# A hybrid decoder layer on one core: page rows of 512 in two rings, keys and C rows loaded a step ahead, the last tile by halves

## The chip, the cores and the metric

The kernel runs on one core of one Trainium2 chip. Its time is the device time of an execution in microseconds (us). A core has a matrix engine (TensorE, PE in the profile, with its weight loads as PEld), VectorE (DVE), ScalarE (ACT), GpSimd (POOL) and SyncE (SP), which here only issues transfers between the chip's memory and the core's buffer.

## The reference

One layer of a hybrid decoder: a diagonal state space branch (S5) and a gated DeltaNet branch run side by side on the same normalised input, are merged by gates, and a SwiGLU block follows. Everything is float32. 2048 prompt positions with 16 meta tokens ahead, and 8 running sequences of 4 tokens; the width is 1024, the inner width of the SwiGLU 2816.

```python
def layer(x, h_re, h_im, s_gdn, conv_buf, splits, lp):
    hn = rms_norm(x, lp['norm_mix_pre'])
    proj = hn @ lp['w_in']
    ...
    y_s5, h_re_n, h_im_n = s5_mix(u, h_re, h_im, ...)
    gs = jax.nn.gelu(y_s5)
    br_a = (gs @ lp['w_s5_glu_a']) * jax.nn.sigmoid(gs @ lp['w_s5_glu_b'])
    qkv_c, conv_new = short_conv(qkv, conv_buf, lp['gdn_conv_w'])
    ...
    o_seg, S = gdn_segment(q, k, v, g, beta, S)          # in chunks of 64
    o = rms_norm(o, lp['gdn_norm']) * jax.nn.silu(zf)
    br_b = o.reshape(b, l, GDN_VW).astype(x.dtype) @ lp['w_gdn_out']
    mix = (jax.nn.sigmoid(ga) * br_a + jax.nn.sigmoid(gb) * br_b) @ lp['w_out']
    x = x + rms_norm(mix, lp['norm_mix_post'])
    f = rms_norm(x, lp['norm_ffn_pre'])
    f = (jax.nn.silu(f @ lp['w_ffn_gate']) * (f @ lp['w_ffn_up'])) @ lp['w_ffn_down']
    x = x + rms_norm(f, lp['norm_ffn_post'])
    return x, h_re_n, h_im_n, S, conv_new
```

## The kernel before

The prompt is cut into four blocks of 512 columns; block 0 has 48 more (16 meta tokens and 32 sample tokens). Each float32 operand of the large products is split into a high and a low part, and a product is made of three: high by high, high by low, low by high (`mm3`, L157 to L161; in the profile three lines in turn, all of one shape). Weight units of 1024 columns come by `wload` (L131): SP loads `wr`, ACT writes the high part, POOL and DVE write half of the low part each into `wu`, a unit of a ring (`Ring`, L56) over the free places of several pools.

**Five stages** follow each other on PE.

- *Projections*, 0 to 1281 us. `p1` goes through groups of output tiles (u, qkv, gate) and, for each, over two blocks. A block's normalised features stand as "pages" (`pages`, L1247), sixteen tiles of two rows by 560 columns, the pool `pg`: four for the high parts `pgh` and four for the low ones `pgl`, for two blocks at a time. They are made by `p1_features` and `to_features` (L243): transposes on PE into `pst`, high part by ACT, low part by DVE. Beside the products, four queues of generators are advanced by `tick` (L1779) at given rates: features of later blocks, `gdn_alpha` (keys and decay: `kTa`, `E`, the products `psk`, and `Z`, stored to `m_d`), the tables of S5 (`s5_setup`, whose loop over two halves loads rows of C as `ctl`, L1021, and transposes them, L1044), and the chunks of the delta rule (`gdn_chunk` with `px`, `X`, and `o_out` with `pT`, L732). One core's engines work through their own lists in order, which the build fixes: what stands behind a waiting instruction on an engine's list waits too, SP's list of transfers included. All plain loads and stores named here are on SP's list.
- *Merge*, 1281 to 1595 us: products of the S5 outputs and of the DeltaNet outputs with three weights (`psga`, `psgb`, `psgo`). Their inputs are pages again (`p2_prep`, L1251).
- *Way out*, 1595 to 1796 us (`psr`, L1377 to L1380): the merged features are the stationary operand, weights are streamed.
- *Gate and up*, 1796 to 2696 us (`psf`), 348 or 344 columns a product, with sums and differences of operands in big buffers on one side of the core's memory (`gr`, `xp`, `fr`, `ae`, `am0`, `am1`). Results are stored to `h_d`.
- *Down*, 2700 to 3215 us (`down`, `down_tiles` L1630): two halves of the rows, four groups of the inner width. `hr` loads a piece of `h_d`, ACT and DVE split it to `hh` and `hl` (stationary), the streamed operand is the weight unit, and sums collect in `facc`. Twelve weight units lie in `wp3`, in the place of gate and up's buffers, from address 122848 per partition on. After the last group of a row tile its squares are summed (ACT), `rsqrt` (L102 to L109) takes twelve small DVE instructions, one DVE instruction scales the tile, and POOL adds it to `y_prompt` in the chip's memory by an accumulating transfer (L1669).

Of the kernel before, what the change touches and what calls it, by code (L numbers as in the profile page):

```python
# [24 lines left out]
H = 4  # L25
# [17 lines left out]
GW = 348  # L43
PAIRS = ((0, 348), (696, 348), (1392, 344))
# [7 lines left out]
def ap_of(t, off, dims):  # L52
    return bass.AP(tensor=t.tensor, offset=t.offset + off, ap=[list(d) for d in dims])
# [19 lines left out]
class Trunk:  # L73
# [169 lines left out]
    def to_features(self, ys, gain, hi, lo):  # L243
# [4 lines left out]
        for k0 in range(0, 8, 2):  # L248
            ps = self.pt.tile([P, 2, 256], F32, tag="pt", name="pst")
# [323 lines left out]
    def gdn_alpha(self, b):  # L573
# [7 lines left out]
        zs = []  # L581
        for i, (ci, nt, c0) in enumerate(ch):
            kT = self.gd.tile([P, H, P], F32, tag="al", bufs=3, name="kTa")[:, :, :nt]
            nc.sync.dma_start(kT, ap_of(self.qkv_d, 512 * QW + c0, [[QW, P], [P * QW, H], [1, nt]]))
            e = self.decay_load(ci, nt, self.gd.tile([P, H, P], F32, tag="al", bufs=3, name="E"))
# [9 lines left out]
            z = self.gd.tile([P, H, P], F32, tag="al", bufs=3, name="Z")[:nt, :, :nt]  # L595
# [115 lines left out]
    def o_out(self, o, qn, lo, hi, col):  # L711
# [16 lines left out]
        yield  # L728
        pT = self.gp.tile([P, H, P], F32, tag="gp", name="pT")
# [7 lines left out]
    def gdn_chunk(self, ci, c0):  # L737
# [9 lines left out]
        for a in (0, 64):  # L747
            for h in range(H):
                mm(px[a:a + 32, h, 0:32], M[a + 32:a + 64, h, a:a + 32], V[a + 32:a + 64, h])
            v.tensor_copy(X[a:a + 32], px[a:a + 32, :, 0:32])  # L750
# [130 lines left out]
    def s5_setup(self):  # L881
# [118 lines left out]
        nc.sync.dma_start(ld[:16], ap_of(io["s5_D"], 0, [[1, 16], [16, G]]))  # L1000

# [6 lines left out]
        for hf in range(2):  # L1008
# [8 lines left out]
            cts = []  # L1017
            for nm in ("s5_C_re", "s5_C_im"):
                ct = self.c2("ctl")[:, :256].rearrange("p (q k e) -> p q k e", q=2, k=2)
                for k in range(2):  # L1020
                    nc.sync.dma_start(ct[:, :, k], ap_of(io[nm], h0 * 16 * 64, [[64, P], [P * 64, 2], [1, 64]]))  # L1021
                cts.append(ct)
# [25 lines left out]
            for g0 in range(h0, h0 + 16, 4):  # L1048
# [24 lines left out]
                outer(V2, (CR, CI), (R2, R1), "n", 1, 9)  # L1073
                nc.sync.dma_start(self.wv_d[gs, :, 3].rearrange("g p (t c) -> p g t c", c=16), V2)
# [171 lines left out]
    def pages(self, n):  # L1246
        new = lambda nm: [self.pg.tile([P, 2, PW], F32R, tag="pg", name=nm) for _ in range(n)]  # L1247
        return new("pgh"), new("pgl")

    def p2_prep(self, b):  # L1250
# [4 lines left out]
        oh, ol = self.pages(2)  # L1255
# [8 lines left out]
        sh, sl = self.pages(2)  # L1264
# [365 lines left out]
    def down_tiles(self, grp, k0, n, wd, gi, last):  # L1630
        nc, v = self.nc, self.nc.vector
        c0 = grp[0][2]
# [11 lines left out]
        for a, r, c in grp:  # L1644
            both = wide and gi < last
            rr = 2 * r if both else r
            cl = slice(c - c0, c - c0 + rr)
            for half in range(2):
# [7 lines left out]
                if gi == 0:  # L1656
                    nc.scalar.activation(a[:rr, cs], ps, AF.Copy)
                else:
                    v.tensor_add(a[:rr, cs], a[:rr, cs], ps)
            if wide and gi == last - 1:  # L1660
                t = self.lw.tile([SMP, D], F32, tag="lw", name="lows")
                nc.sync.dma_start(t, a[r:2 * r])
                nc.gpsimd.tensor_add(a[:r], a[:r], t)
            if gi == last:
# [4 lines left out]
                nc.gpsimd.dma_start(dst, a[:r], accum_op=OP.add)  # L1669

# [14 lines left out]
    def run(self):  # L1685
# [16 lines left out]
        with ExitStack() as lo:  # L1702
            self.wr = self.pool("wr", 2, lo)
            self.wp.add(self.pool("wp", 3, lo), 3)
            with ExitStack() as pmx, ExitStack() as pgx:
                self.pg = self.pool("pg", 16, pgx, side="right")
# [44 lines left out]
        with ExitStack() as ph:  # L1751
# [9 lines left out]
            self.wp.add(self.pool("wp3", 12, ph, side="right", **kw), 12)  # L1761
# [73 lines left out]
    def p1_features(self, b):  # L1835

        hi, lo = self.pages(4)
        for grp in self.pairs(self.load_tokens(b, True)):
            self.normed(grp, [t for t, _, _ in grp])
            yield  # L1840
            yield from self.to_features(grp, self.g_mix, hi, lo)
        self.xs[b] = hi, lo
# [130 lines left out]
```

## Time and profile before

| what | us |
|---|---|
| median of three runs | 3237.43 (3235.34 to 3238.28) |
| the profiled execution's own time | 3230.07 |
| its span, first to last instruction | 3228.3 |
| PE busy in the span | 3095.1 |
| PE busy in projections, merge, way out, gate and up, down | 1193.95, 302.24, 198.29, 885.52, 515.14 |
| the stages' lengths | 1281, 314, 201, 900, 519, and an end of 13.3 |
| granted clock of PE, mean over the span | 0.978 |

Times below are us from the start of the span of that one execution. A group row reads: line, engine, operation, output and inputs by the program's names, shapes, number of instructions; after the bar the busy time, the mean length in ns, and the idle time just before them with what ended it. A wait row reads: engine and tile with its line, the engine and instruction that ended the wait, total us, times, longest. A window row reads: stretch, its length, busy time of PE, PEld, DVE, ACT, POOL with instructions in brackets, PE's granted clock (1.00 is full), the share of the time that the transfer engines were busy, GB/s. A row of the timeline or of the chain starts with its start and length in us. "SPq" is the issuing of SP's transfers.

### The profile page before, as it was taken

How to read it: one execution, taken by the hardware profiler on the slowest of the kernel's cores; microseconds unless marked ns; L12 is line 12 of the kernel's file. 1: busy time of each engine (PE TensorE's matmuls, PEld its weight loads, DVE VectorE, ACT ScalarE, POOL GpSimd, SP SyncE). 2: the span in 40 equal slices, each digit the busy share in tenths (PEclk: the TensorE clock that was granted, in tenths of full speed). 3: DMA queues.
4: the chain of work that ended last, by engine and by line, in shares of the span. 5: the costliest groups of instructions: out<-in, count | busy, mean ns of one | idle time of the engine just before them, and what ended most of it. 6: DMA issues, size and time to landing. Idle time of an engine off the chain costs nothing.

```text
span 3228.3 us, 47504 instructions
## 1 busy us (share of the span) xinstructions
PE 3095.1 (96%) x17461; PEld 2719.5 (84%) x17461; DVE 2047.1 (63%) x4674; ACT 1127.2 (35%) x1952; POOL 892.9 (28%) x907
## 2 busy tenths in 40 slices
PE   7998989999999999899999899999999999999998
PEld 6887887877777887888788799999999998887776
DVE  6888864557798645644456777777777773245235
ACT  4642222433333224311244444444444444223211
POOL 1133431113332211300211444434434444121110
PEclk9999998999999999999999999999999999999999
DMA  4335556445556645544555533343323335235214
GB/s 120 122 98 164 137 157 179 116 111 141 158 172 180 169 120 149 173 132 134 162 175 190 171 105 105 105 123 106 105 88 105 105 105 174 83 107 133 88 57 70
DMA packets 460552, 419.29 MB, mean 130 GB/s; under 512 B 112330, under 2 KB 384906, under 8 KB 460320
## 3 DMA queue, kind: packets, MB, share of 16 engines
q1 hardware_dynamic: 450048, 382.18, 40.6%
q0 software_dynamic: 10272, 34.09, 3.8%
q8 instruction: 137, 2.24, 0.3%
q14 instruction: 95, 0.78, 0.1%
HBM read 288.27 MB, written 127.65 MB: 129 GB/s over the span
## 4 chain that ended last, share of the span: by engine, by line
PE 67%; DVE 15%; issue 10%; DMA 5%; ACT 2%; POOL 1%; SPq 0%; POOLq 0%; DVEq 0%; ACTq 0%
PE psf L161 9%; PE psf L159 9%; PE psf L160 9%; PE psr L1652 3%; PE psr L1653 3%; PE psr L1655 2%; PE psg L159 2%; PE psg L161 2%; PE psg L160 2%; DVE cy L391 2%; PE psr L1377 2%; PE psr L1378 2%; PE psr L1380 1%; PE psq L159 1%; PE psq L161 1%
## 5 line engine op out<-in xcount | busy, mean ns | idle before, releaser
L159 PE MATMUL psf<-xh,ah 128*128 128x348 f32 (+1 forms) x1848 | 595.0, 322 | 6.2 <-ACT sn L1546 4.5
L160 PE MATMUL psf<-xl,ah 128*128 128x348 f32 (+1 forms) x1848 | 593.8, 321 | 0.0
L161 PE MATMUL psf<-xh,al 128*128 128x348 f32 (+1 forms) x1848 | 593.5, 321 | 0.0
L146 POOL TENSOR_TENSOR wu<-wr,wu 128x512 fp32r<-128x512 f32 x136 | 218.1, 1606 | 690.0 <-ACT wu L144 664.1
L159 PEld LDWEIGHTS psf<-xh,ah 128*128 128x128 f32 x1848 | 348.3, 188 | 8.0 <-ACT sn L1546 5.4
L161 PEld LDWEIGHTS psf<-xh,al 128*128 128x128 f32 x1848 | 348.4, 189 | 0.2 <-DVE al L1486 0.2
L160 PEld LDWEIGHTS psf<-xl,ah 128*128 128x128 f32 x1848 | 348.4, 189 | 0.0
L159 PE MATMUL psg<-pgh,wu 128*128 128x512 f32 (+2 forms) x800 | 301.2, 377 | 1.2 <-ACT gt L1223 1.2
L1652 PE MATMUL psr<-wu,hh 128*128 128x512 f32 (+2 forms) x748 | 295.9, 396 | 3.9 <-ACT hh L1638 3.9
L1653 PE MATMUL psr<-wu,hh 128*128 128x512 f32 (+2 forms) x748 | 295.8, 395 | 0.0
L161 PE MATMUL psg<-pgh,wu 128*128 128x512 f32 (+2 forms) x800 | 290.3, 363 | 4.0 <-DVE wu L147 4.0
L160 PE MATMUL psg<-pgl,wu 128*128 128x512 f32 (+2 forms) x800 | 289.2, 362 | 0.0
L1655 PE MATMUL psr<-wu,hl 128*128 128x512 f32 x704 | 277.3, 395 | 0.0
L147 DVE TENSOR_TENSOR wu<-wr,wu 128x512 fp32r<-128x512 f32 x136 | 121.0, 891 | 130.7 <-ACT wu L144 127.8
L144 ACT ACTIVATE wu<-wr 128x1024 fp32r<-128x1024 f32 x136 | 142.6, 1054 | 133.8 <-DMA wr<-w_ffn_down 48.8
L159 PE MATMUL psq<-pgh,wu 128*128 128x512 f32 (+2 forms) x480 | 183.1, 381 | 4.6 <-ACT gt L1223 4.0
L161 PEld LDWEIGHTS psg<-pgh,wu 128*128 128x128 f32 x800 | 156.0, 195 | 28.7 <-DVE wu L147 4.2
L159 PEld LDWEIGHTS psg<-pgh,wu 128*128 128x128 f32 x800 | 155.8, 195 | 26.6 <-issue 6.1
L160 PE MATMUL psq<-pgl,wu 128*128 128x512 f32 (+2 forms) x480 | 174.4, 363 | 0.0
L161 PE MATMUL psq<-pgh,wu 128*128 128x512 f32 (+2 forms) x480 | 173.7, 362 | 0.0
L1652 PEld LDWEIGHTS psr<-wu,hh 128*128 128x128 f32 (+2 forms) x748 | 138.8, 186 | 39.8 <-ACT hh L1638 4.2
L160 PEld LDWEIGHTS psg<-pgl,wu 128*128 128x128 f32 x800 | 155.9, 195 | 19.2 <-issue 0.2
(498 smaller groups left out, 6721.3 us busy)
## 6 DMA issues: line engine op xcount, KB each, us to landing
wr<-w_in SPq DMA_DIRECT2D x72, 512.0 KB
araw<-w_ffn_gate SPq DMA_DIRECT2D x31, 1024.0 KB
araw<-w_ffn_up SPq DMA_DIRECT2D x31, 1024.0 KB
wr<-w_ffn_down SPq DMA_DIRECT2D x44, 512.0 KB
zg_d<-gt SPq DMA_DIRECT2D x80, 256.0 KB
h_d<-hm SPq DMA_DIRECT2D x44, 348.0 KB
qkv_d<-cy SPq DMA_DIRECT2D x48, 256.0 KB
hr<-h_d SPq DMA_DIRECT2D x16, 768.0 KB
```

Of the source, the lines that this page charges most:

```text
L144: nc.scalar.activation(hi[:, :n], raw[:, :n], AF.Copy)
L146: nc.gpsimd.tensor_sub(lo[:, :c], raw[:, :c], hi[:, :c].bitcast(F32))
L147: nc.vector.tensor_sub(lo[:, c:n], raw[:, c:n], hi[:, c:n].bitcast(F32))
L159: t.matmul(ps, wh, xh, start=first, stop=False, **kw)
L160: t.matmul(ps, wh, xl, start=False, stop=False, **kw)
L161: t.matmul(ps, wl, xh, start=False, stop=last, **kw)
L391: nc.vector.scalar_tensor_tensor(yp, raw[:, j:j + np_], w[j], yp, op0=OP.mult, op1=OP.add)
L1377: nc.tensor.matmul(o, hi[:, k, :rr], wh[:, cs], start=i == 0, stop=False)
L1378: nc.tensor.matmul(o, hi[:, k, :rr], wl[:, cs], start=False, stop=wide and i == 7)
L1652: nc.tensor.matmul(ps, hi[:, k, cl], wh[:, cs], start=k == 0, stop=False)
L1653: nc.tensor.matmul(ps, hi[:, k, cl], wl[:, cs], start=False, stop=both and k == n - 1)
L1655: nc.tensor.matmul(ps, lo[:, k, c - c0:c - c0 + r], wh[:, cs], start=False, stop=k == n - 1)
```

## The change

**Pages.** Instead of sixteen small tiles there are two rings of two tiles of eight rows, one ring for even and one for odd blocks. Block 0's rows are 576 columns apart, the others' 512 (before 560). In `p2_prep` high and low part of one operand share one tile.

**Down.** The tile of pool `lw` becomes 96 columns longer, by which the pools behind it (`hr`, `hh`, `ac3`, `rows3`) begin 384 bytes further on. The twelve units become two pools of six; the first six now lie where gate and up's `fr`, `xp` and `gr` were.

**Loads ahead.** `s5_setup` loads the C rows of its first half before its loop and those of its second half in the first half's last step, in one tile of the pool `tm`. `gdn_alpha` loads keys and decay rows one chunk ahead, in five buffers instead of three; the first chunk of each block is loaded at its start.

**Order.** `gdn_chunk` makes both halves of `px` before the two copies to `X`; `o_out` pauses three times instead of twice ahead of `pT`; block 0's transposes also use the PSUM buffers of the pool `gp`. **The last row tile** ends by halves (`down_end`).

```diff
-    def to_features(self, ys, gain, hi, lo):
+    def to_features(self, ys, gain, hi, lo, wide):
 
         nc = self.nc
         c0 = ys[0][2]
         w = sum(r for _, r, _ in ys)
         for k0 in range(0, 8, 2):
-            ps = self.pt.tile([P, 2, 256], F32, tag="pt", name="pst")
+            pool, tag = (self.gp, "gp") if wide and k0 else (self.pt, "pt")
+            ps = pool.tile([P, 2, 256], F32, tag=tag, name="pst")
...
-        zs = []
+        new = lambda nm: self.gd.tile([P, H, P], F32, tag="al", bufs=5, name=nm)
+        def load(ci, nt, c0):
+            kT = new("kTa")[:, :, :nt]
+            nc.sync.dma_start(kT, ap_of(self.qkv_d, 512 * QW + c0, [[QW, P], [P * QW, H], [1, nt]]))
+            return kT, self.decay_load(ci, nt, new("E"))
+        nxt = load(*ch[0])
         for i, (ci, nt, c0) in enumerate(ch):
-            kT = self.gd.tile([P, H, P], F32, tag="al", bufs=3, name="kTa")[:, :, :nt]
-            nc.sync.dma_start(kT, ap_of(self.qkv_d, 512 * QW + c0, [[QW, P], [P * QW, H], [1, nt]]))
-            e = self.decay_load(ci, nt, self.gd.tile([P, H, P], F32, tag="al", bufs=3, name="E"))
+            kT, e = nxt
+            nxt = load(*ch[i + 1]) if i + 1 < n else None
...
-            z = self.gd.tile([P, H, P], F32, tag="al", bufs=3, name="Z")[:nt, :, :nt]
+            z = new("Z")[:nt, :, :nt]
...
         yield
         yield
+        yield
         pT = self.gp.tile([P, H, P], F32, tag="gp", name="pT")
...
         for a in (0, 64):
             for h in range(H):
                 mm(px[a:a + 32, h, 0:32], M[a + 32:a + 64, h, a:a + 32], V[a + 32:a + 64, h])
+        for a in (0, 64):
             v.tensor_copy(X[a:a + 32], px[a:a + 32, :, 0:32])
...
+        def rows_c(h0):
+            t = self.tm.tile([P, D], F32, tag="tm", name="ctl")[:, :512].rearrange("p (i q k e) -> p i q k e", i=2, q=2, k=2)
+            for i, nm in enumerate(("s5_C_re", "s5_C_im")):
+                for k in range(2):
+                    nc.sync.dma_start(t[:, i, :, k], ap_of(io[nm], h0 * 16 * 64, [[64, P], [P * 64, 2], [1, 64]]))
+            return [t[:, i] for i in range(2)]
+        nxt = rows_c(0)
 
...
-            cts = []
-            for nm in ("s5_C_re", "s5_C_im"):
-                ct = self.c2("ctl")[:, :256].rearrange("p (q k e) -> p q k e", q=2, k=2)
-                for k in range(2):
-                    nc.sync.dma_start(ct[:, :, k], ap_of(io[nm], h0 * 16 * 64, [[64, P], [P * 64, 2], [1, 64]]))
-                cts.append(ct)
+            cts = nxt
             yield
...
+                if g0 == 12:
+                    nxt = rows_c(16)
...
-    def pages(self, n):
-        new = lambda nm: [self.pg.tile([P, 2, PW], F32R, tag="pg", name=nm) for _ in range(n)]
-        return new("pgh"), new("pgl")
+    def pages(self, b, n):
+
+        pitch = PITCH if b == 0 else BLK
+        out = []
+        for nm in ("pgh", "pgl"):
+            if n == 4 or nm == "pgh":
+                t = self.pg.tile([P, 8 * (PITCH if b % 2 == 0 else BLK)], F32R, tag=f"pg{b % 2}", bufs=2, name=nm)
+                rows = t[:, :8 * pitch].rearrange("p (k c) -> p k c", k=8)
+                at = 0
+            out.append([rows[:, at + 2 * i:at + 2 * i + 2] for i in range(n)])
+            at += 2 * n
+        return out
 
...
-        oh, ol = self.pages(2)
+        oh, ol = self.pages(b, 2)
...
+            if gi == last and c + r == SEQ:
+                end = self.down_end(a, r, c)
+                next(end)
...
-                t = self.lw.tile([SMP, D], F32, tag="lw", name="lows")
+                t = self.lw.tile([SMP, D + 96], F32, tag="lw", name="lows")[:, :D]
...
-            if gi == last:
+            if gi == last and not end:
...
+    def down_end(self, a, r, c):
+        nc, v = self.nc, self.nc.vector
+        rows = lambda cs: ap_of(self.io["y_prompt"], c * D + cs.start, [[D, r], [1, cs.stop - cs.start]])
+        halves = [slice(0, BLK), slice(BLK, D)]
+        y = self.lw.tile([P, D + 96], F32, tag="lw", name="yl")[:, :D]
+        nc.sync.dma_start(y, rows(slice(0, D)))
+        g = self.ac.tile([P, D], F32, tag="ac", name="fg")
+        ss = self.small.tile([P, 2], F32, tag="sse", bufs=1, name="sse")
+        rs = self.small.tile([P, 1], F32, tag="rse", bufs=1, name="rse")
+        yield
+        for i, cs in enumerate(halves):
+            j = self.c2("sq").bitcast(BF16)[:, :BLK]
+            nc.scalar.activation(j, a[:, cs], AF.Square, accum_out=ss[:, i:i + 1])
+            v.tensor_mul(g[:, cs], a[:, cs], self.r_fpost[:, cs])
+            if i == 0:
+                yield
+        v.tensor_add(ss[:, 0:1], ss[:, 0:1], ss[:, 1:2])
+        self.rsqrt(rs, ss[:, 0:1], 1.0 / D, EPS, "e")
+        for cs in halves:
+            v.scalar_tensor_tensor(g[:, cs], g[:, cs], rs[:, 0:1], y[:, cs], op0=OP.mult, op1=OP.add)
+            nc.sync.dma_start(rows(cs), g[:, cs])
+        yield
...
-                self.pg = self.pool("pg", 16, pgx, side="right")
+                self.pg = self.pool("pg", 2, pgx, side="right")
...
-            self.wp.add(self.pool("wp3", 12, ph, side="right", **kw), 12)
+            self.wp.add(self.pool("wp3", 6, ph, side="right", **kw), 6)
+            self.wp.add(self.pool("wp5", 6, ph, side="right", **kw), 6)
```

Where the change moves instructions, three places show it. **SP's list in `gdn_alpha`, where block 0's chunks end and block 1's begin** (`Z` goes to `m_d`, `kTa` and `E` are a chunk's keys and decay rows, `zg_d`, `wv_d`, `tt_d`, `qkv_d` are results). Before:

```order
L1228 DMA zg_d<-gt 128x512
L607 DMA m_d<-Z 128x512
L1229 DMA zg_d<-gt 128x32
L584 DMA kTa<-qkv_d 128x4x128
L562 DMA E<-gct_d 128x512
L1105 DMA wv_d<-s5w 128x4x256
L1074 DMA wv_d<-V_3477 128x4x128
```

After:

```order
L1240 DMA zg_d<-gt 128x512
L613 DMA m_d<-Z 128x512
L1241 DMA zg_d<-gt 128x32
L586 DMA kTa<-qkv_d 128x4x128
L564 DMA E<-gct_d 128x512
L586 DMA kTa<-qkv_d 128x4x128
L564 DMA E<-gct_d 128x512
L1117 DMA wv_d<-s5w 128x4x256
L1086 DMA wv_d<-V_3468 128x4x128
```

The loads of block 1's first two chunks now stand together; the store of `Z` is still ahead of both.

**PE's list at a chunk of the delta rule**, in the middle of the products `psu` (`px` are the 32x32 products of the chunk, `vp` transposes of its values, `pT` the output's transposes of the chunk before). Before:

```order
L161 MATMUL psu<-pgh,wu 128x304
L740 MATMUL px<-U_6167,M 32x32 x4
L680 MATMUL vp<-ident,xv 128x128 x4
L740 MATMUL px<-U_6167,M 32x32 x4
L159 MATMUL psu<-pgh,wu 128x512
L160 MATMUL psu<-pgl,wu 128x512
L161 MATMUL psu<-pgh,wu 128x512
L732 MATMUL pT<-ident,o 128x128 x4
```

After, the place of `px`, and then the place of `pT`:

```order
L161 MATMUL psu<-pgl,wu 128x512
L162 MATMUL psu<-pgh,wu 128x512
L747 MATMUL px<-U_6165,M 32x32 x8
L686 MATMUL vp<-ident,xv 128x128 x4
L160 MATMUL psu<-pgh,wu 128x512
L161 MATMUL psu<-pgl,wu 128x512
```

```order
L747 MATMUL po<-X,T_6111 32x32 x2
L747 MATMUL po<-T_6111,X 32x32
L747 MATMUL po<-X,T_6111 32x32 x2
L747 MATMUL po<-T_6111,X 32x32
L699 MATMUL pq<-kq 128x128 x4
L739 MATMUL pT<-ident,o 128x128 x4
L747 MATMUL px<-U,M 64x64 x4
L747 MATMUL pk<-S,kq 128x128 x4
```

The two times four `px` have become eight in a row; `pT`, which stood three products behind them, now stands behind the chunk's `po` and `pq`, some twelve `psu` products later.

**SP's list at the start of down** (`wr` are loads of its weights, `hr` its first activations, `h_d` the last stores of gate and up). Before:

```order
L142 DMA wr<-w_ffn_down 128x1024
L1559 DMA h_d<-hm 128x688
L142 DMA wr<-w_ffn_down 128x1024 x3
L1636 DMA hr<-h_d 128x6x256
L142 DMA wr<-w_ffn_down 128x1024
L1559 DMA h_d<-hm 128x688
L1767 DMA row<-norm_ffn_post 128x1024
```

After:

```order
L143 DMA wr<-w_ffn_down 128x1024
L1581 DMA h_d<-hm 128x688
L143 DMA wr<-w_ffn_down 128x1024 x5
L1659 DMA hr<-h_d 128x6x256 x2
L143 DMA wr<-w_ffn_down 128x1024
L1581 DMA h_d<-hm 128x688
L143 DMA wr<-w_ffn_down 128x1024
L1581 DMA h_d<-hm 128x688
L1820 DMA row<-norm_ffn_post 128x1024
L1659 DMA hr<-h_d 128x6x256 x2
```

Six weight loads and two `hr` now stand ahead of the last stores of `h_d` that had been behind four weight loads and one `hr`; and on **ACT's list** the splits of the six units (`wu`) stand among the last steps of gate and up (`sn`, `th`). Before:

```order
L1546 ACTIVATE sn<-psf 128x344 x4
L1555 ACTIVATE th<-su 128x344
L144 ACTIVATE wu<-wr 128x1024 x2
L1546 ACTIVATE sn<-psf 128x344
L1555 ACTIVATE th<-psf 128x344
L144 ACTIVATE wu<-wr 128x1024
L1555 ACTIVATE th<-su 128x344
L144 ACTIVATE wu<-wr 128x1024
L1638 ACTIVATE hh<-hr 128x1536
L144 ACTIVATE wu<-wr 128x1024 x2
```

After:

```order
L1568 ACTIVATE sn<-psf 128x344
L145 ACTIVATE wu<-wr 128x1024 x2
L1568 ACTIVATE sn<-psf 128x344 x2
L145 ACTIVATE wu<-wr 128x1024 x2
L1568 ACTIVATE sn<-psf 128x344
L1577 ACTIVATE th<-su 128x344
L145 ACTIVATE wu<-wr 128x1024
L1568 ACTIVATE sn<-psf 128x344
L145 ACTIVATE wu<-wr 128x1024
L1577 ACTIVATE th<-psf 128x344
L1577 ACTIVATE th<-su 128x344
L1661 ACTIVATE hh<-hr 128x1536 x2
```

The first `hh` had one `wu` between itself and the last `th`; now both `hh` follow that `th` at once.

More of the change, by code (lines that the diff above doesn't have):

```diff
@@ L43 @@
 GW = 348
+PITCH = 576
 PAIRS = ((0, 348), (696, 348), (1392, 344))
@@ L1262, in p2_prep @@
                        self.g_gdn[:, 0:1])
-        sh, sl = self.pages(2)
+        sh, sl = self.pages(b, 2)
         for m in range(4):
@@ L1631, in down_tiles @@
         nc, v = self.nc, self.nc.vector
+        end = None
         c0 = grp[0][2]
@@ L1659, in down_tiles @@
                     v.tensor_add(a[:rr, cs], a[:rr, cs], ps)
+                if end:
+                    next(end)
             if wide and gi == last - 1:
-                t = self.lw.tile([SMP, D], F32, tag="lw", name="lows")
+                t = self.lw.tile([SMP, D + 96], F32, tag="lw", name="lows")[:, :D]
                 nc.sync.dma_start(t, a[r:2 * r])
                 nc.gpsimd.tensor_add(a[:r], a[:r], t)
-            if gi == last:
+            if gi == last and not end:
                 rs = self.rstd_of([(a, r, c)], "f")
@@ L1835, in p1_features @@
     def p1_features(self, b):
-        hi, lo = self.pages(4)
+        hi, lo = self.pages(b, 4)
         for grp in self.pairs(self.load_tokens(b, True)):
@@ L1840, in p1_features @@
             yield
-            yield from self.to_features(grp, self.g_mix, hi, lo)
+            yield from self.to_features(grp, self.g_mix, hi, lo, b == 0)
         self.xs[b] = hi, lo
```

## The prediction

> **What bounds the kernel now.** The page first: the share of each engine, and the chain of work that ended last.
>
> ```profile
> PE 3095.1 (96%) x17461; PEld 2719.5 (84%) x17461; DVE 2047.1 (63%) x4674; ACT 1127.2 (35%) x1952; POOL 892.9 (28%) x907
> PE 67%; DVE 15%; issue 10%; DMA 5%; ACT 2%; POOL 1%; SPq 0%; POOLq 0%; DVEq 0%; ACTq 0%
> ```
>
> TensorE (PE) is busy for 96% of the span, so there are only two places to win: the 3228.3 - 3095.1 = 133 us in which it stands, and the spacing of its products. Next, PE's waits:
>
> ```profile
> PE psk L590 <- DMA kTa<-qkv_d: 9.5, 1, 9.5
> PE px L740 <- DVE X L750: 9.1, 7, 3.1
> PE pT L732 <- DVE o L726: 8.7, 4, 6.0
> PE pst L1044 <- DMA ctl<-s_C_re: 6.0, 2, 4.2
> PE pst L1044 <- DMA ctl<-s_C_im: 5.2, 2, 4.9
> PE pst L252 <- issue: 4.8, 1, 4.8
> PE psr L1652 <- ACT hh L1638: 3.9, 1, 3.9
> ```
>
> Each row gives the total, the number and the longest wait in us. These seven are the waits that the change is made at; together 47.2 us. To see what stands round them I read windows of 10 us (busy time of PE, PEld, DVE, ACT and POOL with instructions in brackets, then the granted clock, the DMA share and GB/s):
>
> ```profile
> 225.00:235.00 10.00, 5.56 (x26) 4.74 (x25) 7.54 (x39) 1.65 (x2) 5.20 (x8) 0.67 0.52 117
> 290.00:300.00 10.00, 3.62 (x23) 2.82 (x21) 9.48 (x26) 1.74 (x5) 5.70 (x6) 1.00 0.28 89
> 300.00:310.00 10.00, 5.10 (x22) 5.10 (x23) 6.98 (x24) 2.56 (x4) 2.87 (x2) 0.50 0.76 231
> 360.00:370.00 10.00, 5.80 (x24) 4.98 (x25) 7.12 (x12) 1.82 (x4) 9.62 (x12) 0.66 0.28 91
> 580.00:590.00 10.00, 6.86 (x47) 5.65 (x46) 6.37 (x23) 2.43 (x7) 1.27 (x1) 0.84 0.36 82
> ```
>
> Behind a long wait PE is granted half its clock: 0.50 throughout 300 to 310. A clock of 0.67 means about 3.3 us more work than time, 0.66 the same. So a removed wait gives back its own length and up to half of the slow stretch. But at 290 to 300 DVE is busy for 9.48 of 10 us: there PE waits for DVE in one form or another, and a gain on PE alone is partly taken back.
>
> Last, the spacing of 128x512 products, the commonest shape. A window counts whatever overlaps it; a product is listed with 0.39 to 0.40 us, so some 1.7 of each count began before the window. The rows are way out, merge and down (twice):
>
> ```profile
> 1725.50:1745.50 20.00, 20.00 (x90) 16.50 (x89) 10.27 (x20) 7.11 (x12) 2.54 (x4) 1.00 0.53 181
> 1450.00:1550.00 100.00, 100.00 (x433) 80.99 (x432) 45.24 (x63) 17.17 (x23) 11.49 (x15) 1.00 0.43 129
> 2710.00:2830.00 120.00, 120.00 (x518) 97.30 (x517) 34.51 (x34) 31.88 (x35) 20.74 (x12) 1.00 0.34 107
> 2965.00:3085.00 120.00, 120.00 (x518) 96.04 (x517) 27.03 (x30) 23.70 (x28) 10.73 (x6) 1.00 0.27 79
> ```
>
> At full clock: 20/88.3 = 226.5 ns in way out, 100/431.3 = 231.9 in merge, 120/516.3 = 232.4 in down. PE never waits in any of them, and way out is the fastest under the highest DMA share (0.53), so transfers don't explain it. What differs is where operands begin. In the built program of before, the moving operand's address less that of the next stationary one, modulo 512 bytes, is 0 in way out, 384 in down and takes eight values in merge and in the projections.
>
> **The change, part by part.** Sums stand against the profiled execution (3230.07 us, span 3228.3), which is 7.4 us below the median of 3237.43.
>
> *Equal places (page rows of 512, the longer row in down).* In the program of after that difference is 0 in down and for nearly all 512-column products of the projections and merge; block 0's narrower ones get 0 or 256. If the place sets the spacing, these reach 226.5.
>
> ```profile
> L1652 PE MATMUL psr<-wu,hh 128*128 128x512 f32 (+2 forms) x748 | 295.9, 396 | 3.9 <-ACT hh L1638 3.9
> L1655 PE MATMUL psr<-wu,hl 128*128 128x512 f32 x704 | 277.3, 395 | 0.0
> L160 PE MATMUL psgo<-pgl,wu 128*128 128x512 f32 x96 | 38.0, 396 | 0.0
> L160 PE MATMUL psg<-pgl,wu 128*128 128x512 f32 x479 | 192.9, 403 | 0.0
> 1061.06 0.40 PE L159 MATMUL psg<-pgh,wu 128*128 128x512 f32 x1
> 1065.64 0.39 PE L161 MATMUL psg<-pgh,wu 128*128 128x512 f32 x1
> ```
>
> Down: L1652, L1653 (as many) and L1655 make 2200 products by 232.4 - 226.5 = 5.9 ns, 13.0 us. Merge: three tiles (psga, psgb, psgo) by three lines by 96, 864 by 5.4, 4.7. Projections: psg 3x479 (the fifth and sixth row are the first and last start of 20 unbroken intervals: 4.58/20 = 229 ns); with psq and psu, which have 3x286 and 3x96 of the same form, 2583 by 2.5 makes 6.5, of which I take 5.5, since the DVE-bound stretches absorb some. Together **23 us** (0 if place doesn't matter; the ceiling is this sum plus 1).
>
> Here a rule speaks against the change. The Trainium skill, "TensorE: Matmul & The Clock Gate" (Part 2, Step-by-step, the drain step), says that PE reads its streamed operand and its weights through two independent SBUF ports. By it the two could not meet, and this term would be 0 and the sum 41 instead of 64. The rows of way out and down don't agree with a single spacing for one shape, but they don't show the cause either; so the rule stays as a rival below.
>
> *C rows and decay rows ahead.* Before, PE stands 4.2 us (225 to 235) and 4.9 (about 360) for C rows that the SyncE (SP) queue issues only when they are needed, and 9.5 for kTa. That one is issued behind another SP instruction:
>
> ```profile
> 300.18 0.88 DVE Z L606 x3
> 301.08 0.32 SPq L607
> 301.96 2.90 DMA kTa<-qkv_d
> ```
>
> SP's store of Z (L607) waits for DVE, and the load behind it takes 2.90. In the order of after this Z store is still ahead of this kTa load, which is the first of its block's chunks and so not loaded ahead: the wait moves, and shrinks only as far as DVE arrives earlier. The C rows of both halves do go far ahead. The price is a buffer: the ctl tile occupies one of the four work buffers (tm) from its load till its transposes, and SP's later loads queue behind any one that waits for such a buffer; no row shows such a wait, so I bound it by 0 and by the 9.5 of the kTa row, and take 0, since the other users of these buffers (bm, bt, s5k) hold theirs only from a load to the next few instructions. The pages too are now released eight rows at a time instead of two, to the block after next; with the same bounds I take 0, as PE has no row of a wait for a page buffer now and the last unit of a block reads all of its rows anyway. First C half and kTa: bounds 4 (the first C wait alone) and 4.2 + 3.3 + 9.5 + 5 (half of the 10 slow us) = 22; DVE at 9.48 of 10 keeps me low, **10**. Second half: 4.9 and the other 1.8 of the C_re row, with 3.4 of clock, bounds 4 and 10; DVE has 2.9 us free at 360 to 370, so **8**.
>
> *px before both X copies; pT later.* px waited seven times, 9.1 us, and 1.6 of clock at 580 to 590 (0.84). Eight products in a row need one release instead of two, and the copies then run side by side with PE's other work: **7** (bounds 0 and 10.7). The added yield puts the output's transposes pT some 8 us of PE work later in PE's order.
>
> ```profile
> 1329.39 1.11 PE L732 MATMUL pT<-ident,o 128*128 128x128 f32 x4 [5.96 <-DVE o L726]
> 30.00:40.00 10.00, 6.13 (x24) 5.13 (x25) 7.65 (x38) 6.48 (x18) 0.00 (x0) 0.52 0.48 127
> 2695.00:2705.00 10.00, 6.11 (x22) 4.78 (x21) 5.24 (x6) 3.60 (x3) 5.30 (x4) 0.83 0.93 307
> ```
>
> Of pT's 8.7 us the longest, 5.96 before 1329.39, keeps its place in the order, since nothing is left there to put ahead of it; the other 2.7 go, with up to half of a slow spell such as the one behind px: **4** (bounds 0 and 6).
>
> *Start.* All 16 transposes of block 0's first tiles now stand ahead of its products, on a wider PSUM supply, and the small tile's loads ahead of two weight loads. The 4.8 (issue) row and the 10 us at clock 0.52 (second row above) hang on it, though the same loads and DVE's first splits come first in either order: **3** (bounds 0 and 4.8 + 4.8).
>
> *Down's start.* Before:
>
> ```profile
> 2672.33 19.15 SPq L142 DMA_DIRECT2D wr<-w_ffn_down  x3
> 2691.53 6.59 DMA hr<-h_d
> 2698.14 1.49 ACT hh L1638
> ```
>
> Three weight loads sit 19.15 us in SP's queue until ACT's and POOL's splits free their buffers, and the first activations (hr) come behind. Six units now lie where gate_up's buffers end early, their splits stand among its last steps, and hr is ahead of what waits. The first product can follow the last of gate_up: 3.9 of wait less 0.4 for the release, and 1.5 of the slow clock behind it (0.83 of 10 us, 1.7), **5** (bounds 0 and 5.6).
>
> *Last tile by halves.*
>
> ```profile
> 3214.42 0.40 PE L1655 MATMUL psr<-wu,hl 128*128 128x512 f32 x1
> 3215.64 1.06 ACT L233 ACTIVATE sq<-facc 128x1024 bf16<-128x1024 f32 x1 [5.82 <-DVE facc L1659]
> 3216.82 0.15 DVE L102 TENSOR_SCALAR rsx<-ss 128x1 f32<-128x1 f32 x1 [1.27 <-ACT sq L233]
> 3219.14 1.28 DVE L1666 SCALAR_TENSOR_TENSOR facc<-facc,rs,row 128x1024 f32<-128x1024 f32 x1
> 3220.71 0.86 POOL L1669 DMA_DIRECT2D y_prompt<-facc  x1 [5.64 <-DVE facc L1666]
> ```
>
> Before, 3228.3 - 3220.71 = 7.6 us pass from POOL's issue to the end. After: half a square saves 0.5, one small add costs 0.2; rstd stays at 2.3; two final halves cost as much as the whole (1.3), the last store goes out at about 3220.5 by SP, whose issue and landing I put at 0.4 + 2.9 (kTa's row, the same 256 KB): end at 3223.8, **4.5** (bounds: 0, and 6 if the store lands in 2).
>
> Sum: 23 + 10 + 8 + 7 + 4 + 3 + 5 + 4.5 = **64.5**. 3230.1 - 64.5 = 3165.6 on the profiled execution's scale, with its 7.4 us **3173** as a median.
>
> **Rivals.**
> 1. *Place doesn't matter* (each product takes its columns and a fixed cost, whatever its addresses). For it: the projections run at 229 with eight different places, hardly worse than way out. Against: down and merge, steadily 5 ns over way out. Gain 41.5, time **3196**. It is the case that the rule of the Trainium skill named above describes.
> 2. *The projection stage is DVE's.* PE's waits there only move to the next DVE result (9.48 of 10 busy). The equal places of merge and down, the start and both ends remain: 13 + 4.7 + 3 + 5 + 4.5 = 30, time **3207**. Against: DVE is busy for only 7.0 to 7.5 of 10 in the other windows.
> 3. *Slower: equal places collide.* If both operands at the same place get in each other's way, every 512-column product of the three stages goes up, to the worst interval that down shows at its place:
>
> ```profile
> 2968.74 0.40 PE L1655 MATMUL psr<-wu,hl 128*128 128x512 f32 x1
> 2968.98 0.40 PE L1652 MATMUL psr<-wu,hh 128*128 128x512 f32 x1
> ```
>
> 240 ns: 2200 x 7.6 + 864 x 8.1 + 2583 x 11 = 52 us lost against 41.5 won, **3248**. It decides from 7.3 ns more per product on (41.5/5647). Against: way out has equal places and the shortest spacing.
> 4. *The change doesn't do what it says*, the equal places being cancelled by another tile's shift and the C rows by a full buffer: some 20 us, **3217**.
>
> **How the numbers follow.** Forecast 0.52, rival 1 0.18, rival 2 0.17, rival 3 0.05, rival 4 0.08. The range takes the forecast with its bounds (3148 if the stalls go to their upper bounds) and rivals 1 and 2: **3146 to 3208**; outside lie rivals 3 and 4 and the edge of rival 2. A measurement of this kernel tells 0.2% (6.5 us) from no change: faster 0.92, same 0.03, slower 0.05, since only rival 3 and a part of rival 4 come near or over the old time.
>
> **What would show it.** Windows inside down and merge at 226 to 227 ns per product (x518 becoming x531 in 120 us of down), else rival 1. No waits for ctl and hh in PE's list; px's wait below 2. kTa's wait may stay; if the waits of the list are replaced by equal ones for DVE between 200 and 400 us and the merge begins within 10 us of its old place, rival 2. The end less than 10 us after the last product. The prediction is wrong if products space out beyond 233, or if SP waits for work buffers in the projections.

## The result, and the profile after

| | before | after |
|---|---|---|
| median, us | 3236.39 (4 runs, 3235.02 to 3238.28) | 3194.57 (4 runs, 3190.25 to 3197.77) |
| ratio | | 0.987, 95% interval 0.9852 to 0.9887 |
| profiled execution, us (span) | 3230.07 (3228.3) | 3190.25 (3188.5) |
| PE busy, us | 3095.1 | 3061.1 |

The kernel is 42 us faster. The time lies in the forecast range, 21 us above the point forecast of 3173. That it lies close to the 3196 of the first rival is chance: that rival goes without the gain from places, which came, and it has all the other gains, of which more than half did not come. The page's first lines after:

```profile
PE 3061.1 (96%) x17461; PEld 2710.2 (85%) x17461; DVE 2047.4 (64%) x4678; ACT 1128.7 (35%) x1956; POOL 894.4 (28%) x906
PE 74%; DVE 15%; DMA 4%; issue 2%; ACT 2%; SPq 1%; POOL 1%; DVEq 0%; ACTq 0%; POOLq 0%
```

PE is busy for 34 us less with the same 17461 instructions, so most of the gain is products that take less time, by closer spacing or by a higher clock (its mean went from 0.978 to 0.981), and not shorter waits: the standing time went from 133 to 127 us, and the chain's share of PE from 67 to 74%. The windows of merge and of down (twice), in the form shown before (third column is PE with its count):

```profile
1500.00:1550.00 50.00, 50.00 (x222) 41.39 (x221) 22.90 (x31) 10.67 (x13) 13.44 (x13) 1.00 0.49 158
2690.00:2810.00 120.00, 120.00 (x532) 99.34 (x531) 33.87 (x36) 30.56 (x34) 21.15 (x12) 1.00 0.29 88
2940.00:3060.00 120.00, 120.00 (x531) 97.74 (x530) 30.71 (x34) 25.35 (x30) 13.59 (x8) 1.00 0.23 68
```

Less the 1.7 that began before each window: 50/220.3 = 227.0 ns in merge (before 231.9), 120/530.3 and 120/529.3 = 226.3 and 226.7 ns in down (before 232.4). PE's waits, the rows that answer to those shown of before and the two that grew:

```profile
PE pT L739 <- DVE o L732: 10.6, 4, 6.0
PE psq L160 <- ACT gt L1235: 10.1, 4, 5.8
PE psk L596 <- DMA kTa<-qkv_d: 9.8, 1, 9.8
PE psg L160 <- ACT gt L1235: 6.1, 2, 4.3
PE psr L1678 <- ACT hh L1661: 3.0, 1, 3.0
PE po L747 <- DVE X L758: 1.8, 2, 1.0
```

The waits for ctl (11.2 us before) are gone, and px's 9.1 have become 1.8 for the next step, po. But kTa's wait is what it was, hh's is 0.9 shorter, pT's rose from 8.7 to 10.6, and ACT's gt (tiles of the gate) now costs 10.1 and 6.1. Before, it cost less:

```profile
PE psq L159 <- ACT gt L1223: 4.0, 2, 2.2
PE psg L159 <- ACT gt L1223: 1.2, 1, 1.2
```

To see what the C rows brought, take two fixed points in PE's list, the 301st and the 2101st of the products that `mm3` makes. In one window between them, before and then after:

```profile
94.50:474.90 380.40, 345.44 (x2090) 305.79 (x2089) 314.38 (x1010) 139.31 (x256) 126.93 (x140) 0.95 0.48 137
...
88.60:469.60 381.00, 344.97 (x2090) 306.86 (x2089) 311.39 (x1010) 141.95 (x258) 128.62 (x140) 0.95 0.49 136
```

380.4 and 381.0 us, with equal busy times: all that was removed there came back. The stretch varies little from one execution to another: in twelve of the fourteen profiled executions of this document (the two above and one of each run below) it takes 379.7 to 381.9 us; the other two are named below. What the changed kernel is ahead at the end of the stretch, 5.3 us, it had at its beginning.

Two more places. Down's start, on PE, then on ACT, on DVE and on POOL:

```profile
2671.75 0.31 PE L162 MATMUL psf<-xh,al 128*128 128x344 f32 x1
2675.06 0.80 PE L1678 MATMUL psr<-wu,hh 128*128 128x512 f32 x1 [2.99 <-ACT hh L1661]
...
2670.13 1.06 ACT L145 ACTIVATE wu<-wr 128x1024 fp32r<-128x1024 f32 x1 [2.14 <-DMA wr<-w_ffn_down]
2671.10 0.44 ACT L1577 ACTIVATE th<-psf 128x344 f32<-128x344 f32 x1
2673.14 0.49 ACT L1577 ACTIVATE th<-su 128x344 f32<-128x344 f32 x1 [1.60 <-POOL wu L147]
2673.54 2.84 ACT L1661 ACTIVATE hh<-hr 128x1536 fp32r<-128x1536 f32 x2
...
2671.23 0.69 DVE L148 TENSOR_TENSOR wu<-wr,wu 128x512 fp32r<-128x512 f32 x1 [2.43 <-ACT wu L145]
2672.26 0.51 DVE L1572 TENSOR_TENSOR su<-psf,sn 128x344 f32<-128x344 f32 x1
...
2671.28 1.77 POOL L147 TENSOR_TENSOR wu<-wr,wu 128x512 fp32r<-128x512 f32 x1 [0.85 <-ACT wu L145]
```

hh does follow the last th at once, as the order said. But that th begins 1.4 us after PE's last product began. It reads the su that DVE ends at 2672.77, and on DVE that step stands behind DVE's share of a weight unit's split, which in turn waited for ACT's share and for the unit's load (the 2.14 us in the row of ACT's wu). For the last 0.4 us the profile names POOL's share, which ends at 2673.05. hh itself takes another 1.5, so PE stands 3.0 us instead of 3.9. And the end:

```profile
3179.19 0.39 PE L1681 MATMUL psr<-wu,hl 128*128 128x512 f32 x1
3180.40 0.63 ACT L1712 ACTIVATE sq<-facc 128x512 bf16<-128x512 f32 x1 [2.31 <-DVE facc L1685]
3183.66 1.42 DVE L1719 SCALAR_TENSOR_TENSOR fg<-fg,rse,yl 128x512 f32<-128x512 f32 x2
3184.44 1.01 SPq L1720 DMA_DIRECT2D y_prompt<-fg  x2
```

From the last product's start to the end of the span 9.3 us (3188.5 - 3179.2), before 13.9 (3228.3 - 3214.4).

### The profile page after: what moved, and what is told of

Its sections match the earlier page's. It is cut to its first block, busy times and chain, and to the rows that moved or that the text cites. A ratio compares the mean times of both kernels' runs of the same rounds, so it can differ in the third digit from the quotient of the medians.

```text
span 3188.5 us, 47491 instructions
## 1 busy us (share of the span) xinstructions
PE 3061.1 (96%) x17461; PEld 2710.2 (85%) x17461; DVE 2047.4 (64%) x4678; ACT 1128.7 (35%) x1956; POOL 894.4 (28%) x906
## 4 chain that ended last, share of the span: by engine, by line
PE 74%; DVE 15%; DMA 4%; issue 2%; ACT 2%; SPq 1%; POOL 1%; DVEq 0%; ACTq 0%; POOLq 0%
PE psf L162 9%; PE psf L160 9%; PE psf L161 9%; PE psr L1678 5%; PE psr L1679 5%; PE psr L1681 5%; PE psg L160 2%; PE psg L162 2%; PE psg L161 2%; DVE cy L393 2%; PE psr L1399 2%; PE psr L1400 2%; PE psr L1402 1%; PE psq L160 1%; PE psga L161 1%
## 5 line engine op out<-in xcount | busy, mean ns | idle before, releaser
L1678 PE MATMUL psr<-wu,hh 128*128 128x512 f32 (+2 forms) x748 | 292.8, 391 | 3.0 <-ACT hh L1661 3.0
L1679 PE MATMUL psr<-wu,hh 128*128 128x512 f32 (+2 forms) x748 | 292.5, 391 | 0.0
L1681 PE MATMUL psr<-wu,hl 128*128 128x512 f32 x704 | 273.9, 390 | 0.0
L160 PE MATMUL psq<-pgh,wu 128*128 128x512 f32 (+2 forms) x480 | 181.5, 378 | 11.1 <-ACT gt L1235 10.1
L1508 POOL TENSOR_TENSOR al<-R,ah 128x1024 fp32r<-128x1024 f32 x62 | 160.9, 2596 | 37.6 <-ACT ah L1507 37.5
```

The costliest lines, as they stand in the source:

```text
L160: t.matmul(ps, wh, xh, start=first, stop=False, **kw)
L1508: eng.tensor_sub(flat(lo), x, flat(hi).bitcast(F32))
L1678: nc.tensor.matmul(ps, hi[:, k, cl], wh[:, cs], start=k == 0, stop=False)
L1679: nc.tensor.matmul(ps, hi[:, k, cl], wl[:, cs], start=False, stop=both and k == n - 1)
L1681: nc.tensor.matmul(ps, lo[:, k, c - c0:c - c0 + r], wh[:, cs], start=False, stop=k == n - 1)
```

## The experiments

All twelve are compared with the kernel before on the same chip; its median was 3233.97, 3237.3 and 3234.61 us in the three sets. Where a difference in us is given, it is the difference of two ratios times 3235; with intervals of 0.15 to 0.2% to either side such a difference is uncertain by 7 to 9 us. Where a length between two instructions is given for several kernels, it is from the one profiled execution of each. The changed kernel was run again in the second set.

**c_after.** No edit.

> The changed kernel again, as the base of this set: 0.987 of the time before, some 3192.

Measured: 3194.15 us, ratio 0.9871 (0.985 to 0.9892). It is the base below.

### Places

**a_noplace**, only addresses altered: in the built program the lists of all five engines are those of the changed kernel, instruction for instruction.

```diff
-PITCH = 576
+PITCH = 560
...
-        pitch = PITCH if b == 0 else BLK
+        pitch = PITCH if b == 0 else BLK + 16
...
-                t = self.lw.tile([SMP, D + 96], F32, tag="lw", name="lows")[:, :D]
+                t = self.lw.tile([SMP, D], F32, tag="lw", name="lows")[:, :D]
```

> The changed kernel with the old places alone: page rows of 560 in block 0 and 528 in the other blocks, and down's longer row taken back; every engine's order stays that of the changed kernel. Place theory: down's products go from 226.9 ns back to 232.3 (about 2200 by 5.4 = 11.8 us), merge's 864 by 4.9 (4.2) and the projections' by up to 2.5 (5.7): about 21.7 us above the changed kernel's 3194.6, so 3216. Rival, that the spacing came from other parts of the change (other order, other buffers): products stay at 227 and the time within 3 us of 3195.

Measured: 3215.48 us, ratio 0.9939 (0.9927 to 0.9952), 22 us more than the changed kernel. Its windows in merge and down:

```profile
1500.00:1550.00 50.00, 50.00 (x218) 40.53 (x217) 21.99 (x30) 9.74 (x12) 10.96 (x11) 1.00 0.42 133
2700.00:2820.00 120.00, 120.00 (x518) 97.30 (x517) 33.73 (x35) 30.18 (x34) 20.16 (x12) 1.00 0.28 87
```

50/216.3 = 231.2 and 120/516.3 = 232.4 ns, the spacing of the kernel before. (The places in down are those of before; the page rows, 528 columns apart instead of 560, have other places than before, but unequal ones too.)

**e_places**, the other way round: the kernel before with the new `pages` and the longer row in down alone.

```diff
-        oh, ol = self.pages(2)
+        oh, ol = self.pages(b, 2)
...
-                t = self.lw.tile([SMP, D], F32, tag="lw", name="lows")
+                t = self.lw.tile([SMP, D + 96], F32, tag="lw", name="lows")[:, :D]
```

> The kernel before with the new pages (rows of 576 and 512 in two rings) and the longer row in down alone. Place theory: 226.9 ns in down and merge as in the changed kernel, 3236.4 - 21.7 = 3215. If the projections' stage is bound by VectorE, only down's and merge's 16 us: 3220. Rival, that place counts only together with the other parts: 3236.

Measured: 3210.68 us, ratio 0.9932 (0.9918 to 0.9945): 22 us less than before. Down there:

```profile
2710.00:2830.00 120.00, 120.00 (x531) 99.37 (x531) 37.04 (x37) 32.17 (x34) 21.71 (x14) 1.00 0.33 103
```

120/529.3 = 226.7 ns. Added to the old kernel and taken from the new one, the places are worth the same 22 us, over half of the gain. (The new pages also come free eight rows at a time, so here the lists aren't quite those of before; a_noplace is the clean one of the two.)

**m_abs64**, another place, still equal:

```diff
-        raw = self.wr.tile([P, 1024], F32, tag="wr", name="wr")
+        raw = self.wr.tile([P, self.wrw], F32, tag="wr", name="wr")[:, :1024]
...
+            self.wrw = 1040
             self.wr = self.pool("wr3", 2, ph, side="right", **kw)
```

with `D + 96` made `D + 64`.

> The changed kernel with both operands of down moved: weights and hh, hl begin at 352 modulo 512 instead of 480, still equal to each other. If the difference counts: 226.9 ns as in the changed kernel. If a certain place counts (480): 231 to 233.

Measured: one run, 3190.65 us.

```profile
2700.00:2820.00 120.00, 120.00 (x531) 99.45 (x530) 36.57 (x39) 31.73 (x34) 21.40 (x13) 1.00 0.32 101
```

226.7 ns: no certain place is needed.

**m_map**, one of the operands spread over all eight differences:

```diff
-            lo = self.hh.tile([P, 6, 256], F32R, tag="hl", name="hl")
+            lo = self.hh.tile([P, 6, 272], F32R, tag="hl", name="hl")[:, :, :256]
```

> The changed kernel with the rows of hl (the low part of down's stationary operand) 272 columns apart instead of 256, so that in one run the product ahead of each hl load (L1679) meets it at all eight differences modulo 512, from 0 to 448 in steps of 64, and the other products at 0. If only equality counts: 226.9 ns at 0 and one higher value at all seven others, near 232. If the spacing goes up with the distance: a ramp from 227 on. If place is not the cause: 227 at all eight.

Measured: one run, 3199.74 us, and none of the three. The mean interval from the start of an L1679 to the next product, by the difference of its streamed operand to the hl loaded meanwhile, with counts:

```
difference   0      64     128    192    256    320    384    448
ns         229.9  228.1  229.3  227.2  227.7  226.0  232.1  227.0
count       159     64     64     32     64     96    138    127
```

L1678, whose streamed operand keeps difference 0 to both of its stationary ones, the one it uses and the one loaded meanwhile, became slower too: 229.9 ns, in the changed kernel 227.1. L1681 went up most, to 232.4 in the mean. The operand loaded meanwhile is at difference 0 there, but the one it uses is the moved hl, and by the difference to that one it goes up and down:

```
difference   0      64     128    192    256    320    384    448
ns         230.6  233.4  232.7  235.0  226.7  232.4  232.9  235.4
count       127     64     64     32     64     96    137    128
```

In down as a whole:

```profile
2700.00:2820.00 120.00, 120.00 (x523) 97.86 (x522) 35.60 (x37) 30.63 (x33) 19.64 (x12) 1.00 0.30 95
```

120/521.3 = 230.2 ns. So the spacing of a product isn't a function of one difference: with up to a third of the stationary operands off the common place all three kinds are slower (L1679 too, 228.8 ns in the mean instead of 226.9). That all three at one place give some 226.7 is shown three times over (changed kernel, e_places, m_abs64). That only equal places do it isn't shown, since some differences in both tables reach the same; why the mixture costs what it does stays open.

### Loads ahead

**a_ctl**

```diff
-            cts = nxt
+            cts = []
+            for nm in ("s5_C_re", "s5_C_im"):
+                ct = self.c2("ctl")[:, :256].rearrange("p (q k e) -> p q k e", q=2, k=2)
...
-                if g0 == 12:
-                    nxt = rows_c(16)
```

> The changed kernel with the C rows loaded where they are needed, as before. My prediction put the two C waits with their slow clock at about 14 of its 18 us for C rows and keys: by it 3209. Theory after the result, that this stretch (200 to 420 us) ends with VectorE's and ScalarE's work whatever PE waits for: the C waits come back in the list (about 10 us) and the waits for gt shrink by as much, so within 3 us of 3194.6.

Measured: 3188.2 us, ratio 0.9861 (0.9848 to 0.9875), 3 us less than the changed kernel, within the intervals. PE's waits there, and the window between the same two products as above:

```profile
PE pst L1051 <- DMA ctl<-s_C_re: 11.2, 2, 7.1
PE psq L160 <- ACT gt L1230: 3.6, 1, 3.6
PE psg L160 <- ACT gt L1230: 0.8, 2, 0.6
...
89.20:470.80 381.60, 345.05 (x2091) 306.77 (x2090) 310.41 (x1009) 141.63 (x258) 126.34 (x140) 0.94 0.49 137
```

The wait for ctl is back with 11.2 us, ACT's gt costs 3.6 and 0.8 instead of 10.1 and 6.1, and the stretch is as long as ever: 381.6 us. One wait stood in for the other.

**a_kta**

```diff
-            kT, e = nxt
-            nxt = load(*ch[i + 1]) if i + 1 < n else None
+            kT = self.gd.tile([P, H, P], F32, tag="al", bufs=3, name="kTa")[:, :, :nt]
+            nc.sync.dma_start(kT, ap_of(self.qkv_d, 512 * QW + c0, [[QW, P], [P * QW, H], [1, nt]]))
+            e = self.decay_load(ci, nt, self.gd.tile([P, H, P], F32, tag="al", bufs=3, name="E"))
```

> The changed kernel with keys and decay rows loaded chunk by chunk in three buffers, as before. By the prediction's share of 4 us: 3199. Theory after the result, that the one long wait (9.8 us) belongs to a first chunk, which is not loaded ahead in either kernel: within 2 us of 3194.6, and the 9.8 stays.

Measured: 3187.67 us, ratio 0.9864 (0.985 to 0.9877).

```profile
PE psk L592 <- DMA kTa<-qkv_d: 15.9, 3, 10.2
```

Two short waits for keys (5.7 us together) come back beside the long one, and cost nothing. Between the 301st and the 2101st product this kernel even takes 375.2 us, less than any run with the keys ahead.

**a_both**, both undone together.

> The changed kernel without both loads ahead (C rows, and keys with decay rows). If each is worth nothing because VectorE and ScalarE set the end of that stretch: the time of the changed kernel, ratio 0.985 to 0.987. If one covers for the other: 7 us or more above it, 0.989 or more.

Measured: 3187.37 us, ratio 0.9856 (0.984 to 0.9873). Neither covers for the other. The three kernels that lack a load ahead are all 2 to 5 us below the changed one, each within the intervals. That the loads ahead don't bring the forecast 18 us is shown. a_both has the lowest ratio of all that were run, and the stretch takes 377.6 us in it. a_kta and a_both are the two runs outside 379.7 to 381.9, so in the changed kernel the keys ahead may even cost 3 to 6 us there; two executions don't prove it, and no run shows why.

### px, pT, the start, the weight pools

**a_px**

```diff
                 mm(px[a:a + 32, h, 0:32], M[a + 32:a + 64, h, a:a + 32], V[a + 32:a + 64, h])
-        for a in (0, 64):
             v.tensor_copy(X[a:a + 32], px[a:a + 32, :, 0:32])
```

> The changed kernel with each half of px followed by its own copy to X, as before. The stretch of PE's products that took 217 us before (475 to 692) takes 206 in the changed kernel. If px made that, its waits (9 us) and the slow clock behind them come back: the stretch at about 214 and the time 7 us (the term of the prediction) above the changed kernel. Rival, that the later pT made it: the px waits come back at 2 to 3 us in all, and the time stays within 2 us.

Measured: 3204.08 us, ratio 0.9904 (0.9885 to 0.9924), 10.7 us more than c_after; the two intervals overlap at their ends. The waits, and the stretch that the expectation names (from the 2101st to the 2701st product), in a_px and in the kernel before:

```profile
PE px L747 <- DVE X L757: 10.2, 8, 3.4
...
469.40:685.30 215.90, 208.06 (x1467) 172.06 (x1465) 111.98 (x352) 73.12 (x186) 37.14 (x53) 0.93 0.56 143
475.00:692.00 217.00, 208.89 (x1482) 174.46 (x1480) 112.06 (x353) 74.23 (x187) 36.60 (x53) 0.94 0.55 143
```

The waits are back, eight with 10.2 us. The stretch alone settles little, because c_after, without these waits, took 215.0 us for it where the profile of the changed kernel has 205.9 (see the last section). All fourteen profiles together tell more: the three with a copy behind each half of px (before, e_places, a_px) take 217.1, 216.3 and 215.9 us, the eleven with px in one go 205.9 to 215.0, with a mean of 209.2. So px in one go is worth some 7 us there.

**a_pT**

```diff
         yield
         yield
-        yield
         pT = self.gp.tile([P, H, P], F32, tag="gp", name="pT")
```

> The changed kernel without the added pause ahead of pT. If the later pT made the gain between 475 and 692 us: 4 us (the term of the prediction) or more above the changed kernel. If px did: within 2 us of it, since the longest wait for pT (6.0) is the same in both kernels.

Measured: 3191.89 us, ratio 0.9871 (0.9847 to 0.9895), the same as c_after to the last digit.

```profile
PE pT L738 <- DVE o L732: 17.4, 9, 6.0
```

The row is 17.4 us here and 10.6 in c_after, and the time doesn't follow the 6.8 us.

**a_wide**

```diff
-            yield from self.to_features(grp, self.g_mix, hi, lo, b == 0)
+            yield from self.to_features(grp, self.g_mix, hi, lo, False)
```

> The changed kernel with block 0's transposes on two PSUM buffers again. The changed kernel is 5.9 us ahead of the one before after its first 300 large products, and keeps it. If the wider supply made that, about 6 us above the changed kernel; if it was the order of the loads, the same as the changed kernel within 2 us.

Measured: 3197.49 us, ratio 0.9883 (0.9865 to 0.9901), 4 us more, less than the intervals tell apart. Of PE's waits, the one that the prediction's term for the start hangs on is back:

```profile
PE pst L254 <- issue: 4.8, 1, 4.8
```

The 301st product starts at 93.7 us. In the other two runs with two buffers it starts at 94.5 (before) and 93.0 (e_places), in the eleven with the wider supply at 87.7 to 90.4; and at the 2101st product the three are still behind all the others (474.1 to 474.9 us against 463.5 to 472.1). So it is the wider supply, with some 4.6 us, and not the loads' order, which a_wide has as changed.

**a_wp**

```diff
-            self.wp.add(self.pool("wp3", 6, ph, side="right", **kw), 6)
-            self.wp.add(self.pool("wp5", 6, ph, side="right", **kw), 6)
+            self.wp.add(self.pool("wp3", 12, ph, side="right", **kw), 12)
```

> The changed kernel with down's twelve weight units in one pool, in the place of gate and up's late buffers, as before. By the prediction's term for down's start, 5 us slower. Theory after the result: the first hh still ends 3 us after the last product of gate and up in the changed kernel (4 before), so the two pools are worth the 1 us of that wait: within 2 us.

Measured: 3192.28 us, ratio 0.9865 (0.985 to 0.9879): no difference.

```profile
PE psr L1678 <- ACT hh L1661: 4.1, 1, 4.1
```

The wait goes from 3.0 to 4.1 us. From the last product of gate and up to the first of down 4.2 to 4.7 us pass in the three runs with one pool (before, e_places, a_wp), 2.1 to 3.6 in the eleven with two: the two pools bring some 1.7 us.

## Why the prediction was right and wrong

| term of the sum | predicted, us | measured, us |
|---|---|---|
| equal places | 23 | 22, both ways |
| C rows and keys ahead | 18 (10 + 8) | 0 (a_both: -4.5, uncertain by 8) |
| px before the copies | 7 | 7 by the traces; 10.7, uncertain by 9 (a_px) |
| pT later | 4 | 0, uncertain by 9 (a_pT) |
| start | 3 | 4.6 by the traces; 4, uncertain by 9 (a_wide) |
| down's start | 5 | 1.7 by the traces; 0, uncertain by 8 (a_wp) |
| last tile by halves | 4.5 | 4.6 by the trace |
| sum | 64.5 | 42 (the whole change) |

With the traces' figures the terms add up to 40 of the 42 us. The measured time is in the range because the range was drawn wide enough for rivals 1 and 2: some 25 us of the sum did not come, nearly all of it in the loads ahead, pT and down's start. (The upper bounds of the stalls, as the prediction lists them, lead to 3146, the lower end of its range, and not to the 3148 named beside it.)

- **Right: the places.** The step that read 226.5 ns in way out against 232.4 in down as a matter of addresses holds: products come 5.7 to 6.1 ns closer in down and 4 to 5 in merge. From its first to its last product down takes 514.7 us in the kernel before and in a_noplace, and 501.3 to 504.1 in the eleven executions with equal places there, so 10.6 to 13.4 us less (forecast 13.0). Merge is 9.0 us shorter in e_places than before, but only 4.2 longer in a_noplace than in the changed kernel (forecast 4.7); what is left of the 22 us, at most 7, falls to the projections (forecast 5.5), where single executions differ by more. The Trainium skill ("TensorE: Matmul & The Clock Gate", Part 2, Step-by-step, the drain step) has PE read its two operands by independent ports; a_noplace, with the same instruction lists and only addresses altered, differs from the changed kernel by 22 us, so here the measurement decides against that rule as a forecast of no effect. Rival 1 fell with it, and rival 3 (collision) too.
- **Wrong: C rows and keys, 18 us.** The step that failed is the reading that a removed wait gives back its length and its slow clock in the stretch from 95 to 475 us. The prediction had the evidence, DVE at 9.48 of 10 us, and discounted the term for it instead of dropping it. What the runs show: the stretch takes 380.4, 381.0 and 381.6 us with the C waits in the list, without them and with them again. This is rival 2 in that stretch, as far as it says that PE's waits only move. What stands in the way after can be read on ACT:

```profile
408.65 0.70 ACT L1235 ACTIVATE gt<-psg 128x256 f32<-128x256 f32 x2 [15.71 <-DVE W L1070]
```

ACT is idle for 15.71 us and ends its wait by DVE's W, a step of the S5 tables; PE waits for the PSUM that this gt empties. A faster arrival of PE only makes that wait longer. gt doesn't read W: in the built program it takes the work buffer of `ow`, an operand that this DVE instruction is the last to read. So it is a buffer that comes free late, on a DVE that is busy for 311 of the 381 us. Whether less work on DVE or more work buffers would shorten the stretch isn't shown: no run changes either. The keys' long wait is as predicted in the order, behind the store of Z:

```profile
295.98 1.14 DVE Z L612 x4
297.13 0.32 SPq L613
297.98 3.59 DMA kTa<-qkv_d
```

so there the mechanism was seen and only the hope that DVE would arrive earlier was wrong. The prediction's own sign for rival 2, a merge that begins within 10 us of its old 1281.1, doesn't decide: it begins at 1265.2 us in the changed kernel's profile and at 1274.6 in c_after's.
- **Rival 2 as a whole** had its 30 us from places, start and ends, and missed px: between 475 and 692 us, where DVE is busy for only half of the time (112 of 206 us in the changed kernel, against 311 of 381 in the stretch ahead), px's waits did count. The rival should have been put as one stretch, not the whole stage.
- **Wrong: pT, 4 us.** The step that failed is that pT's three shorter waits, 2.7 us together, would go: the row rose from 8.7 to 10.6 us. With px in one go and without the later pT it is 17.4 (a_pT), and even that costs no time that the runs can tell.
- **Wrong: down's start, 5 us.** The cover that the prediction named was there: hr in time, hh directly behind th. The step that failed is "the first product can follow the last of gate_up": the splits that moved up stand among the last steps of gate and up on ACT, DVE and POOL, wait there for a weight unit's load, and hold up the last th behind them.
- **Right: px and the start,** 7 against 7 and 4.6 against 3, by the traces, with the medians too coarse to confirm the sizes. **Right: the end,** 4.6 against 4.5.

## What to carry to other kernels

Measure a stretch between two fixed instructions of the bound engine before pricing the waits inside it: where PE depends on an engine that is busy nearly all the time (here DVE, 9.48 of 10 us where the long wait for keys begins), a wait taken away can turn up again at the next thing that engine releases, and the stretch keeps its length. When one shape of product runs at two speeds without any wait, compare where its operands begin; a padded row and other page rows were worth more here than all the loads moved. Where work is moved under cover, look at every engine that does a part of it: here parts of a split on ACT, DVE and POOL came to stand ahead of the last steps that they were to hide behind.

## What the runs showed of the hardware

A product's spacing follows from the places of the operands round it, not from its own alone (m_map: 229.9 ns instead of 227.1 for L1678, whose differences all stayed 0). And two executions of one program differ locally by more than most terms here. The changed kernel and c_after, between the same two products of `mm3` (the 2101st and the 2701st):

```profile
469.60:675.50 205.90, 201.29 (x1467) 168.38 (x1465) 112.08 (x352) 73.32 (x186) 37.16 (x53) 0.96 0.58 147
...
469.60:684.60 215.00, 209.20 (x1465) 173.18 (x1465) 112.12 (x352) 73.17 (x186) 37.15 (x53) 0.92 0.57 143
```

205.9 and 215.0 us, with a mean granted clock of 0.96 and 0.92 and the same instructions. The expectation of a_px took the first for the changed kernel's time in that stretch; one profile can't carry a difference of 9 us there; the medians, or many profiles together, can.
